# RWKV-7 block of a hybrid decoder trunk: small products regrouped by the part of TensorE's array that they use

## The chip, the cores and the metric

The kernel runs on one core of one Trainium2 chip. The metric is the device time of one execution in microseconds (us). Engines are named as in the profile: PE is TensorE (matmuls), PEld its weight loads, DVE VectorE, ACT ScalarE, POOL GpSimd, SP the engine that issues most DMAs. A difference of under about 0.2% (6 us) can't be told from no change here.

## The reference, cut to what matters

The trunk has two layers. Layer 0 runs two recurrent mixers side by side, RWKV-7 (8 heads of 64) and a gated delta rule (4 heads of 128), and adds their output projection to the stream; layer 1 is an RG-LRU; an MLP of width 4096 follows each. There are 1024 prompt tokens and 64 sample tokens (8 sequences of 8), width 1024, all in fp32. The change lies in RWKV-7 alone:

```
w_log = -softplus(-(w0 + tanh(xw) @ w2)) - 0.5        # decay: low-rank product, 64 -> 512
a     = sigmoid(a0 + xa @ a2)                         # in-context rate: low-rank product, 64 -> 512
per token t, per head:                                 # S is 64 x 64
  S = S * w_t + (S a_t) b_t^T + v_t k_t^T
  y_t = S r_t
```

The kernel doesn't go token by token. It cuts the tokens into chunks of 64 and, per chunk and head, works with 64x64 matrices: Gram matrices of (b, k) against (a, r), the inverse of a unit triangular one, u = -(I + L)^-1 x, the output y = (state part) + (part within the chunk), and the next state.

## The kernel before, in words

**Dense work.** Every large product (projections, output projection, MLPs) is made in `dense`: weights and activations are split into a high and a low part (`whi`, `wlo`, `xh`, `xl`), three 128x128 matmuls for each of eight 128-row tiles of the contraction, added in one PSUM bank. Tokens come in columns of 288 or 512.

**The stretch of the recurrences.** From about 270 us to 1130 us the two mixers' recurrences run in stages written out in `ORDER`: `r0 g0 r1 g1 ...`, where `r3` is RWKV's fourth block of 128 tokens, `g3` the delta rule's, and block 8 is the sample. Beside them runs dense work (second halves of the projections, then the output projection and the MLP's first half), which `tick` emits piece by piece. The small products and the dense ones go through the one queue of PE. Their order there is not the source's: the framework that compiles the kernel plans each engine's order beforehand, with the place in the source as priority and its own estimate of when operands and buffers are ready; on the chip each engine then works off its fixed order.

**One RWKV block** (`rwkv_block`, lines 1281 to 1457) treats all heads in lockstep. A pair of heads p (four pairs) shares the 128 partitions: head hh = 0 has partitions 0 to 63, hh = 1 has 64 to 127. A unit u is one chunk of 64 tokens of one pair, so a block of 128 tokens has eight units. Its products, each fp32 matmul of which stands in the trace as two records with a weight load each, are in order:

- decay (line 1316): for each pair, 64 rows of `wa2` (rows 0 to 63) times 128 feature columns, moving 128 tokens. ScalarE turns the bank into `cs`, which becomes the decays `ee`.
- in-context rate (line 1333), after a tick: the same with rows 64 to 127, into a bank of its own, then into `av`.
- Gram (line 1391): per unit and head one matmul with 64 rows and 128 columns ((b, k) by 64), moving 128 columns ((a, r) by 64); four units fill a bank for each head, and VectorE masks them into `ga` and `gr`.
- then `uv`, `xg`, the inverse (`blockinv` through DRAM, levels with `qq`, `tinv`), all in 64x64 products.

**The chain** (`rwkv_chain`, lines 1474 to 1499) then goes through the block's two chunks: xp = state times a (trace: `m<-st,ar`, 64 rows by 64 columns); the solve (`m<-xg,r`), whose result ACT and DVE write into `uv`; the state's increment sp (`m<-uv,bkt`, 128 by 64); two DVE operations that make the new state `st`; and the output y, pair by pair and head by head in one bank `yp`, where the state's part (`m<-ar,st`, 64 rows by 64 columns) is followed at once by the part within the chunk (`m<-gr,uv`, 128 rows by 64 columns).

Banks come from small pools: `psa` (2 banks) for the preparation of both mixers, `psb` (1) for the inverse's levels, `psc` (2) for the chain, `psp` (1) for y and what follows it, `psd` (2) for dense work. A bank is taken again when what reads it is done.

Of the kernel before, what the change touches and what calls it, by code (L numbers as in the profile page):

```python
# [18 lines left out]
P = 128  # L19
# [4 lines left out]
# order of the tokens: the prompt's first half, the sample, the prompt's second half  # L24
# [3 lines left out]
# chunks where the prompt comes first and the sample last  # L28
# [55 lines left out]
# tiles of the recurrences and of the work beside them: columns, ring  # L84
# [12 lines left out]
# tiles of the first MLP's middle that its first half has early: beside the recurrences, after them, in all  # L97
# [3 lines left out]
class Kern:  # L101
# [29 lines left out]
    def wpools(self, es, raw, parts):  # L131
        """places for raw weights and for their parts, beside those that are there"""
        k = len(self.wr)
        self.wr += [self.pool(es, f"wr{k}", raw)] * raw
        self.wp += [self.pool(es, f"wp{k}", parts)] * parts
        self.wn = self.wq = 0
# [9 lines left out]
    # ---- small helpers  # L146
# [9 lines left out]
    def mm(self, out, l, r, start=True, stop=True):  # L156
        return self.nc.tensor.matmul(out, l, r, start=start, stop=stop)  # L157
# [7 lines left out]
    # ---- set-up  # L165
# [10 lines left out]
    def setup_vec(self, vp):  # L176
        """parameters by feature, [P, .]"""
# [40 lines left out]
    def softplus(self, out, x, n, rows=P, pool=None):  # L218
        """out = max(x, 0) + log1p(exp(-|x|)), log1p as 2 atanh(u / (2 + u)); x is overwritten"""
        nc = self.nc  # L220
        pool = pool or self.cst
        ax = pool.tile([P, n], F32, name="spa")[:rows]
        u = pool.tile([P, n], F32, name="spu")[:rows]
        s2 = pool.tile([P, n], F32, name="sps")[:rows]
        self.stt(ax, x, -1.0, x, ALU.mult, ALU.max)
        self.act(u, ax, AF.Exp, scale=-1.0)
        nc.vector.tensor_scalar(ax, u, 2.0, None, op0=ALU.add)
        nc.vector.reciprocal(ax, ax)
        self.tt(u, u, ax, ALU.mult)
        self.tt(s2, u, u, ALU.mult)  # L230
        nc.vector.tensor_scalar(ax, s2, 2.0 / 17, 2.0 / 15, op0=ALU.mult, op1=ALU.add)
        for q in (13, 11, 9, 7, 5, 3, 1):
            self.tt(ax, ax, s2, ALU.mult)
            nc.vector.tensor_scalar(ax, ax, 2.0 / q, None, op0=ALU.add)
        self.tt(ax, ax, u, ALU.mult)
        self.stt(out, x, 0.0, ax, ALU.max, ALU.add)

    # ---- dense machinery
    def wload(self, src, kt, f):
        """src: DRAM [P, kt, f]; returns its two parts by k: [(hi [P, f], lo [P, f])]"""  # L240
        return self.wsplit(self.wraw(src, kt, f), f)
# [25 lines left out]
    def dense(self, w, f0, m, xs, c0, n, head=None):  # L267
        """sum_k w[:, k, f0:f0+m]^T x_k[:, c0:c0+n] into a bank, onto what head leaves there; c0:c0+n lies in
        one of the halves of x"""
# [14 lines left out]
    def xhalf(self, pool, n):  # L284
        """places for half of x_k: [(hi, lo)]"""
        return [tuple(pool.tile([P, n], F32R, name=f"x{p}{k}") for p in "hl") for k in range(8)]
# [13 lines left out]
    def r(self, c0, n):  # L300
        """factors of tokens c0.. of one half"""
        return self.rs[0][:, c0:c0 + n] if c0 < TA else self.rs[1][:, c0 - TA:c0 - TA + n]

    def norm(self, h, wname, l):
        """h times the weights of its norm, split, and in self.rs the factors by token, which the products of h with
        a matrix are still to be multiplied with"""
# [8 lines left out]
    def norm_half(self, hf, h, xs, i, wname, acc, tmp, parts):  # L315
        """half hf of it, in steps; h(f) is a tile of that half, which may be the place of its lower part"""
# [40 lines left out]
    # ---- input  # L357
# [24 lines left out]
    def norm_x(self, xi, h, xs):  # L382
        """first norm of half h of x, by token, and its transpose, split"""
# [36 lines left out]
    # ---- MLP  # L420
    def ahead(self, f0, f1):
        """tiles f0.. of the first MLP's middle, first half of the tokens, to DRAM"""
# [15 lines left out]
    def mlp(self, l, h, xs=None, early=0):  # L438
        """early: so many tiles of the middle lie in DRAM for the first half of the tokens"""
# [31 lines left out]
    # ---- output projection of a mixer: h[f] += sum over its feature tiles, in DRAM as ys [P, k, T]  # L471
    def outproj(self, w_out, xs, ys, h):
        """ys: DRAM [P, 8, T], the prompt first"""
# [15 lines left out]
    # ---- projected rows with their lead-in columns  # L489
    def evac(self, pp, psx, pre, ps, c0, n, b0=0, end=NP, rs=None):  # L490
        """bank of columns c0.. into the prompt tile [P, pre + tokens from b0] and, from column end on, the sample
        tile [P, 8, pre + 8]"""
# [13 lines left out]
    def rows_in(self, dst, src, nt, nr, pool=None):  # L506
        """dst [P, nt, nr] from DRAM rows [nr, nt * P]"""
# [9 lines left out]
    def rows_out(self, src, nt, nr, dsts, pool=None):  # L517
        """src [P, nt, nr] to DRAM rows; dsts: (first row, last row, DRAM rows [., nt * P])"""
# [10 lines left out]
    def tails(self, dst, t, pp, psx, k):  # L529
        """last k columns of the prompt and of each sequence into dst[:, t, :]"""  # L530
# [6 lines left out]
    # ---- RG-LRU layer  # L537
    def lru(self, h):
# [4 lines left out]
        # cL = -8 softplus(-L), stored halved  # L543
# [89 lines left out]
    def conv(self, out, pp, px, wname, nt, t, bias=None):  # L633
        """causal conv of one feature tile; out: tokens of the prompt, then those of the sample if px is there"""
# [13 lines left out]
    # ---- final norm and output  # L648
# [26 lines left out]
    # ---- layer 0: RWKV-7 and gated DeltaNet  # L675
    def scratch(self, name, cols, zero):
        """DRAM scratch for block inverses; zero: an SBUF tile of zeros to fill it with"""
# [5 lines left out]
    def blockinv(self, nb, lb, put, get):  # L683
        """inverses of unit lower 16-blocks, a block a partition: lb [nb, 16 (j), 16 (i)] holds the
        transposed blocks. Leaves them and their transposes in scratch; returns the loaded tiles"""
# [20 lines left out]
    def tick(self, n=1):  # L706
        """emits the next steps of the work that runs beside the recurrences"""
# [103 lines left out]
    def up_start(self):  # L811
        """the first MLP's norm for the first half of the tokens"""
# [9 lines left out]
    def shifted(self, h):  # L822
        """half h of the RWKV projections with their token shift"""
# [39 lines left out]
    def head_squares(self, t, o, m, ss, x):  # L863
        """adds to ss[:, o:o + m] the sums of squares by head that tile t brings; done when the result is called"""
# [13 lines left out]
    def gdn_bg(self):  # L878
        """the delta rule's write strengths and decays by head, to DRAM"""
# [7 lines left out]
    def silu(self, x):  # L887
        """x = y / 2 to y sigmoid(y)"""
# [4 lines left out]
    def delta_in(self, h):  # L893
        """half h of the delta rule's projections: rates, keys, queries and values with their convolution, gates"""
# [29 lines left out]
    def delta_z(self, h):  # L924
        """half h of the delta rule's gates"""
# [13 lines left out]
    def out_half(self, h):  # L939
        """half h of x and the output projection of both mixers, to DRAM"""  # L940
# [34 lines left out]
    def gdn_rates(self, sp):  # L975
        """by token, [P tokens, chunk, head]: write strengths, decays and their sums"""
# [67 lines left out]
    def gdn_block(self, n, b, X):  # L1044
        """everything of 128 tokens (64 of the sample) that needs no state; heads in lockstep"""
# [10 lines left out]
        # by token: keys, values; norms of keys and queries  # L1056
# [27 lines left out]
        # decays D[j, i], Gram matrices  # L1084
# [19 lines left out]
        # (I + N)^-1, transposed  # L1104
# [39 lines left out]
    def gdn_mid(self, b, R, X, p1, p2):  # L1144
        """from k S and q S by token (banks p1, p2): the new values, scaled for the state, and the output"""
# [67 lines left out]
    def gdn_post(self, b, R, X):  # L1213
# [13 lines left out]
        # with s = rq 128^-1/2: out = o s rsqrt(mean((o s)^2) + eps)  # L1227
# [15 lines left out]
    # RWKV: blocks of 128 tokens (64 of the sample), all heads in lockstep; a unit is 64 tokens of a pair of heads  # L1243
# [37 lines left out]
    def rwkv_block(self, n_, b, X):  # L1281
# [26 lines left out]
        # low-rank inputs  # L1308
# [4 lines left out]
        # decay  # L1313
        ps = self.bank()
        for p in range(4):
            self.mm(ps[:, p * n:(p + 1) * n], X["wa2"][:64, p * P:(p + 1) * P], rb[:64, 12])
# [13 lines left out]
        # in-context rate, keys  # L1330
        ps = self.bank()
        for p in range(4):
            self.mm(ps[:, p * n:(p + 1) * n], X["wa2"][64:, p * P:(p + 1) * P], rb[64:, 12])
        av, kk = flat("av"), flat("kk")
        for p in range(4):
            self.act(av[:, p * n:(p + 1) * n], ps[:, p * n:(p + 1) * n], AF.Tanh, bias=self.v("a0h", p), scale=0.5)
# [23 lines left out]
        # bonus  # L1360
# [8 lines left out]
        # values by token; the second head's before, the first head's after  # L1369
# [12 lines left out]
        # Gram matrices [(b|k) j, (a|r) i]; the second head has its k rows first  # L1382
# [3 lines left out]
        for u0 in range(0, U, 4):  # L1386
            gp = [self.bank(), self.bank()]
            for u in range(u0, u0 + 4):
                for hh in range(2):
                    r = slice(hh * 64, hh * 64 + 64)  # L1390
                    self.mm(gp[hh][:, (u - u0) * P:(u - u0 + 1) * P],
                            bk[r, u, hh:hh + 2, :].rearrange("p a t -> p (a t)"),
# [6 lines left out]
        # what the values bring to x  # L1399
# [6 lines left out]
        # b, k by token  # L1406
# [8 lines left out]
        # (I + L)^-1, transposed  # L1415
# [43 lines left out]
    def rwkv_solve(self, R, c, state):  # L1459
        """x = what the values (xg) and the state bring, u = -(I + L)^-1 x of a chunk of every pair, into its rows  # L1460
        of uv"""
# [12 lines left out]
    def rwkv_chain(self, R, st):  # L1474
# [3 lines left out]
        for c in range(2):  # L1478
# [11 lines left out]
            self.tt(sn, s1, lc.to_broadcast([P, 4, 64]), ALU.mult)  # L1490
            for p, hh, q in PH:
                self.mm(yp[q, (2 * p + c) * 64:(2 * p + c + 1) * 64], st[q, p, :], ar[q, 2 * p + c, 1, :], stop=False)
                self.mm(yp[q, (2 * p + c) * 64:(2 * p + c + 1) * 64], uv[:, p, c, hh, :], gr[:, hh, 2 * p + c, :],
                        start=False)
# [6 lines left out]
    def rwkv_states(self):  # L1501
        """states of the sequences for each pair of heads, [(h, k), s, v]"""
# [42 lines left out]
    def rwkv_update(self, R, sts):  # L1545
        """new states of the sequences"""
# [24 lines left out]
    def rwkv_post(self, R, y, X):  # L1571
        """group norm, bonus, gate"""
# [84 lines left out]
```

## Time and profile before

| | |
|---|---|
| Time of the kernel, three runs | 3003.88, 3005.15, 3005.59 us; median 3005.15 |
| The profiled execution | span 3000.1 us from its first to its last instruction; the median of the runs is 5.05 us more |
| PE busy | 2912.1 us, 97% of the span |
| PEld busy | 2549.8 us, 85% |
| DVE / ACT / POOL busy | 1582.5 us (53%) / 1133.3 us (38%) / 132.3 us (4%) |
| Mean granted TensorE clock | 0.980 of full |

Busy time counts an engine's instructions from start to end; a PE that is called busy can be filling and emptying its array between matmuls of different shape. So for PE the distance from one record's start to the next one's says more than the busy share.

### The profile page before, as it was taken

Reading aid. Unit: us, or ns where it says so; the run is one execution under the profiler, and the core shown is the slowest. Engines: PE = TensorE matmul, PEld = TensorE weight load, DVE = VectorE, ACT = ScalarE, POOL = GpSimd, SP = SyncE. Lnnn points to the kernel's source line nnn. Section 1 sums busy time; section 2 is a strip of 40 time slices with the busy share of each in tenths; the row PEclk is TensorE's granted clock in tenths of the full one; section 3 lists DMA queues with packets and bytes.
Section 4 is the critical chain, followed back from the end, with each engine's and each line's share of the span. In section 5 each row is a group of like instructions: output and inputs, shape, how many; then the busy total and the mean of one; then the engine's idle time right before and its main releaser. Section 6 shows DMA issues by size and latency. Waiting matters only on the chain. (4 is left out here: it accounts for less than half of the span.)

```text
span 3000.1 us, 49576 instructions
## 1 busy us (share of the span) xinstructions
PE 2912.1 (97%) x19772; PEld 2549.8 (85%) x19772; DVE 1582.5 (53%) x3383; ACT 1133.3 (38%) x2287; POOL 132.3 (4%) x337
## 2 busy tenths in 40 slices
PE   7999998999999999999999999999999999999997
PEld 6997776667787889988889999888889999999996
DVE  5375666577656563544444335677743333333335
ACT  6355444335345333522222224566441222222222
POOL 2111011110000000000000000000000000000000
PEclk9999998699999999999999999999999999999998
DMA  5344433344344335622221111121421111111112
GB/s 183 114 125 138 111 95 88 92 111 119 108 119 120 98 105 165 197 86 73 79 73 58 46 44 43 47 70 55 150 67 44 43 49 43 43 50 43 43 57 88
DMA packets 419661, 261.04 MB, mean 87 GB/s; under 512 B 95205, under 2 KB 390943, under 8 KB 419430
## 3 DMA queue, kind: packets, MB, share of 16 engines
q1 hardware_dynamic: 413302, 241.90, 27.9%
q0 software_dynamic: 5696, 14.86, 1.6%
q8 instruction: 155, 2.54, 0.3%
q10 hardware_dynamic: 432, 1.11, 0.1%
q14 instruction: 76, 0.62, 0.1%
HBM read 204.07 MB, written 53.73 MB: 86 GB/s over the span
## 5 line engine op out<-in xcount | busy, mean ns | idle before, releaser
L157 PE MATMUL m<-xh,whi 128*128 128x288 f32 (+3 forms) x2984 | 992.1, 333 | 4.6 <-DVE big L151 1.4
L157 PE MATMUL m<-xl,whi 128*128 128x288 f32 (+3 forms) x2984 | 991.4, 333 | 1.3 <-DVE xl L154 0.9
L157 PE MATMUL m<-xh,wlo 128*128 128x288 f32 (+3 forms) x2984 | 981.9, 330 | 0.2
L157 PE MATMUL m<-big,whi 128*128 128x288 f32 (+1 forms) x3072 | 723.2, 327 | 0.0
L148 ACT ACTIVATE whi<-wraw 128x512 fp32r<-128x512 f32 x525 | 329.2, 629 | 1028.1 <-PE m L157 966.9
L157 PEld LDWEIGHTS m<-xh,whi 128*128 128x128 f32 (+1 forms) x2984 | 562.5, 189 | 53.6 <-issue 2.1
L157 PEld LDWEIGHTS m<-xl,whi 128*128 128x128 f32 (+1 forms) x2984 | 563.1, 189 | 44.8 <-issue 1.7
L157 PEld LDWEIGHTS m<-xh,wlo 128*128 128x128 f32 (+1 forms) x2984 | 563.0, 189 | 43.0 <-issue 1.0
L157 PEld LDWEIGHTS m<-big,whi 128*128 128x128 f32 x3072 | 520.2, 188 | 40.4
L151 DVE TENSOR_TENSOR wlo<-wraw,whi 128x512 fp32r<-128x512 f32 x525 | 359.3, 686 | 327.4 <-ACT whi L148 318.4
L157 PE MATMUL m<-big,wlo 128*128 128x288 f32 (+1 forms) x1536 | 501.0, 326 | 0.0
L151 DVE TENSOR_TENSOR h<-h,m 128x288 f32<-128x288 f32 (+1 forms) x408 | 217.0, 532 | 361.9 <-PE m L157 361.9
L157 PEld LDWEIGHTS m<-big,wlo 128*128 128x128 f32 x1536 | 288.3, 188 | 20.6
L148 ACT ACTIVATE mid<-mid 128x288 f32<-128x288 f32 (+1 forms) x202 | 104.1, 518 | 240.3 <-DVE mid L154 203.9
L154 DVE SCALAR_TENSOR_TENSOR mid<-m,rs 128x512 f32<-128x512 f32 (+1 forms) x154 | 85.4, 555 | 177.7 <-PE m L157 177.7
L151 DVE TENSOR_TENSOR big<-mid,big 128x288 fp32r<-128x288 f32 (+2 forms) x170 | 99.4, 585 | 119.8 <-ACT big L148 119.4
L148 ACT ACT_TABLE_LOAD x68 | 87.2, 1283 | 27.9 <-DVE tbtmp L151 13.2
L148 ACT ACTIVATE big<-mid 128x288 fp32r<-128x288 f32 (+2 forms) x170 | 92.7, 545 | 6.5 <-DMA mid<-ma 1.5
L154 DVE SCALAR_TENSOR_TENSOR fpo<-fpp,vt,fpo 128x512 f32<-128x512 f32 x100 | 74.5, 745 | 30.9 <-ACT fpo L148 26.2
L148 ACT ACTIVATE fpp<-m 128x288 f32<-128x288 f32 (+1 forms) x78 | 34.9, 449 | 64.9 <-PE m L157 56.6
L151 DVE TENSOR_TENSOR tbtmp<-lb,tb 32x15 f32<-32x15 f32 (+8 forms) x270 | 51.3, 190 | 5.9 <-DMA lb<-rs 1.6
L151 DVE TENSOR_TENSOR tb<-tb,tbtmp 32x15 f32<-32x15 f32 (+8 forms) x270 | 51.8, 192 | 4.3
(387 smaller groups left out, 2716.9 us busy)
## 6 DMA issues: line engine op xcount, KB each, us to landing
wraw<-mlp_up SPq DMA_DIRECT2D x172, 256.0 KB
wraw<-mlp_down SPq DMA_DIRECT2D x136, 256.0 KB
wraw<-w_in_even SPq DMA_DIRECT2D x120, 256.0 KB
wraw<-w_out_even SPq DMA_DIRECT2D x32, 256.0 KB
wraw<-w_in_odd SPq DMA_DIRECT2D x32, 256.0 KB
wraw<-w_out_odd SPq DMA_DIRECT2D x32, 256.0 KB
in<-rd SPq DMA_DIRECT2D x8, 896.0 KB
mid<-ma SPq DMA_DIRECT2D x22, 288.0 KB
```

Of the source, the lines that this page charges most:

```text
L148: return self.nc.scalar.activation(out, in_, f, **kw)
L151: return self.nc.vector.tensor_tensor(out, a, b, op)
L154: return self.nc.vector.scalar_tensor_tensor(out, a, s, b, op0, op1, **kw)
L157: return self.nc.tensor.matmul(out, l, r, start=start, stop=stop)
```

## The change

Three groups of RWKV's small products are regrouped; what is computed stays the same.

- y: the eight state parts of a chunk go first, in one run, and the eight parts within the chunk after them, in a second run. All sixteen add into one bank, of which only the block's first matmul of each head clears the marks (`start`).
- Gram: each 64x128 product becomes two of 64x64, and they are issued as four quarters of the array: (head 0, b), (head 1, k or b), (head 0, k), (head 1, the other).
- low rank: decay and in-context rate are made in one place, as 64x64 quarters in the same order, into two banks that are taken together; the bank of the rate is read where it was made before.

```diff
-    def mm(self, out, l, r, start=True, stop=True):
-        return self.nc.tensor.matmul(out, l, r, start=start, stop=stop)
+    def mm(self, out, l, r, start=True, stop=True, **kw):
+        return self.nc.tensor.matmul(out, l, r, start=start, stop=stop, **kw)
...
-        ps = self.bank()
+        ps, psr = self.bank(), self.bank()
         for p in range(4):
-            self.mm(ps[:, p * n:(p + 1) * n], X["wa2"][:64, p * P:(p + 1) * P], rb[:64, 12])
+            for k, m in ((0, 0), (1, 1), (0, 1), (1, 0)):
+                f, h64 = p * P + m * 64, slice(k * 64, k * 64 + 64)
+                self.mm((ps, psr)[k][m * 64:(m + 1) * 64, p * n:(p + 1) * n], X["wa2"][h64, f:f + 64], rb[h64, 12])
...
-        ps = self.bank()
-        for p in range(4):
-            self.mm(ps[:, p * n:(p + 1) * n], X["wa2"][64:, p * P:(p + 1) * P], rb[64:, 12])
         av, kk = flat("av"), flat("kk")
         for p in range(4):
-            self.act(av[:, p * n:(p + 1) * n], ps[:, p * n:(p + 1) * n], AF.Tanh, bias=self.v("a0h", p), scale=0.5)
+            self.act(av[:, p * n:(p + 1) * n], psr[:, p * n:(p + 1) * n], AF.Tanh, bias=self.v("a0h", p), scale=0.5)
...
             for u in range(u0, u0 + 4):
-                for hh in range(2):
+                for hh, k in ((0, 0), (1, 1), (0, 1), (1, 0)):
                     r = slice(hh * 64, hh * 64 + 64)
-                    self.mm(gp[hh][:, (u - u0) * P:(u - u0 + 1) * P],
-                            bk[r, u, hh:hh + 2, :].rearrange("p a t -> p (a t)"),
+                    self.mm(gp[hh][k * 64:(k + 1) * 64, (u - u0) * P:(u - u0 + 1) * P], bk[r, u, hh + k, :],
                             ar[r, u].rearrange("p a t -> p (a t)"))
...
+            cols = lambda p: slice((2 * p + c) * 64, (2 * p + c + 1) * 64)
             for p, hh, q in PH:
-                self.mm(yp[q, (2 * p + c) * 64:(2 * p + c + 1) * 64], st[q, p, :], ar[q, 2 * p + c, 1, :], stop=False)
-                self.mm(yp[q, (2 * p + c) * 64:(2 * p + c + 1) * 64], uv[:, p, c, hh, :], gr[:, hh, 2 * p + c, :],
-                        start=False)
+                self.mm(yp[q, cols(p)], st[q, p, :], ar[q, 2 * p + c, 1, :], start=(c == 0 and p == 0), stop=False,
+                        skip_group_check=True)
+            for p, hh, q in PH:
+                self.mm(yp[q, cols(p)], uv[:, p, c, hh, :], gr[:, hh, 2 * p + c, :], start=False,
+                        skip_group_check=True)
```

The rest of the difference is comments that were taken out.

## Rows read from the trace of the kernel before

**Rows 1.** The profile's page: busy engines, then PE and its clock in 40 slices.
```profile
PE 2912.1 (97%) x19772; PEld 2549.8 (85%) x19772; DVE 1582.5 (53%) x3383; ACT 1133.3 (38%) x2287; POOL 132.3 (4%) x337
...
PEclk9999998699999999999999999999999999999998
```
**Rows 2.** Busy time by stretch, with granted clock, DMA share, GB/s at the end.
```profile
270.00:420.00 150.00, 148.65 (x1304) 113.86 (x1304) 96.29 (x264) 74.11 (x182) 13.76 (x27) 1.00 0.43 110
420.00:660.00 240.00, 215.13 (x1496) 154.92 (x1495) 155.46 (x429) 95.88 (x233) 35.91 (x63) 0.85 0.36 90
660.00:1140.00 480.00, 464.80 (x4383) 399.70 (x4383) 308.31 (x847) 215.44 (x544) 20.83 (x37) 0.98 0.43 116
```
**Rows 3.** Who waited for whom, 260 to 1140 us: total, times, longest.
```profile
PE m L157 <- DVE fpp L525: 6.0, 1, 6.0
...
ACT whi L148 <- PE m L157: 76.8, 40, 6.0
ACT uv L148 <- PE m L157: 67.7, 21, 8.2
```
**Rows 4.** Timeline of PE, one chunk's end: start, us, instruction, count of records.
```profile
337.99 0.68 PE L157 MATMUL m<-uv,bkt 128*64 128x64 f32 x14
338.51 0.28 PE L157 MATMUL m<-gr,uv 128*64 128x64 f32 x2
...
339.23 0.33 PE L157 MATMUL m<-ar,st 64*64 64x64 f32 x2
339.48 0.33 PE L157 MATMUL m<-gr,uv 128*64 128x64 f32 x2
339.74 0.33 PE L157 MATMUL m<-ar,st 64*64 64x64 f32 x2
...
341.80 0.50 PE L157 MATMUL m<-xh,wlo 128*128 128x512 f32 x1
342.14 0.40 PE L157 MATMUL m<-xh,whi 128*128 128x512 f32 x1
342.46 0.68 PE L157 MATMUL m<-st,ar 64*64 64x64 f32 x16
342.98 0.28 PE L157 MATMUL m<-ar,st 64*64 64x64 f32 x2
...
343.52 0.39 PE L157 MATMUL m<-xh,wlo 128*128 128x512 f32 x1
343.76 0.39 PE L157 MATMUL m<-xh,whi 128*128 128x512 f32 x1
```
**Rows 5.** Records of PE by tile: count, ns min/median/max, first and last start.
```profile
L157 PE MATMUL m<-gr,uv x272: 221/222/271, 337.1 to 1069.7; 128*64 128x64 f32 x136
...
L157 PE MATMUL m<-ar,bk x272: 271/272/374, 284.4 to 1013.2; 64*128 64x128 f32 x136
...
L157 PE MATMUL m<-in,wa x144: 271/272/524, 271.2 to 965.8; 64*128 64x128 f32 x128, 64*128 64x64 f32 x16
```
**Rows 6.** Timeline of PE: the first block's Gram products.
```profile
284.42 1.86 PE L157 MATMUL m<-ar,bk 64*128 64x128 f32 x16
286.20 0.49 PE L157 MATMUL m<-xh,whi 128*128 128x512 f32 x1
286.63 1.71 PE L157 MATMUL m<-ar,bk 64*128 64x128 f32 x16
288.27 0.50 PE L157 MATMUL m<-xl,whi 128*128 128x512 f32 x1
```
**Rows 7.** Timeline of PE: the second block's low-rank products and what ran between.
```profile
316.17 1.16 PE L157 MATMUL m<-in,wa 64*128 64x128 f32 x8
317.25 0.50 PE L157 MATMUL m<-xh,whi 128*128 128x512 f32 x1
...
322.32 1.14 PE L157 MATMUL m<-tinv,ga 64*64 64x64 f32 x30
...
325.21 1.16 PE L157 MATMUL m<-in,wa 64*128 64x128 f32 x8
326.29 0.91 PE L157 MATMUL m<-qq,tinv 64*64 64x64 f32 x24
```
**Rows 8.** Timeline of DVE: the new state, between sp and xp.
```profile
338.71 0.42 DVE L151 TENSOR_TENSOR s<-m,st 128x256 f32<-128x256 f32 x1 [0.47 <-PE m L157]
...
339.17 0.42 DVE L151 TENSOR_TENSOR st<-s,lam 128x256 f32<-128x256 f32 x1
```

## The prediction

> **What bounds the kernel now.** I read the page first: PE is busy for 97% of the span, DVE for 53% [rows 1]. So time is gained where PE's queue becomes shorter, and the question is whether that holds in the stretch that the change touches, 270 to 1140 us. The windows say that it does: PE is busy for 148.65 + 215.13 + 464.80 = 828.6 of 870 us there, and DVE, the next, for 560 [rows 2]. The waits agree: the longest single wait of PE is 6.0 us, while ACT alone waits 76.8 us for PE to let go of a weight tile and 67.7 us for a solve's result [rows 3]. The 41 us in which PE is not busy lie mostly in 420 to 660 us, round the sample block, where the granted clock is 0.85, that is, part of the stretch runs at the lower of the two levels [rows 2]. I did not trust the busy share further than that, and read the timeline record by record, from start to start, since a busy PE can be one that fills and empties its array.
>
> **y in two runs.** In the timeline of a chunk's end the two shapes of y alternate, two records of one, two of the other. Such a double pair takes 339.74 - 339.23 = 0.51 us for four records, 128 ns each. The same 64x64 shape in an unbroken run takes (342.98 - 342.46) / 16 = 32 ns a record, and the 128x64 shape (338.51 - 337.99) / 14 = 37 ns [rows 4]. So three quarters of y's time is the change of shape and two passes of one product that wait for each other. There are 8 blocks x 2 chunks x 8 = 128 such pairs (272 records of the second part, less 16 of the sample, are 256 [rows 5]), so y costs 128 x 0.51 = 66 us. After the change a chunk has 16 records at 32 ns and 16 at 37 ns, 1.1 us, and at most one more change of shape than now, 0.2 us (dense matmuls follow one another after 343.76 - 343.52 = 0.24 us, and after 0.34 and 0.32 us next to a run of another shape; so a change costs some 0.1 us, and a visit, with both, 0.2 to 0.25 [rows 4]). That is 1.3 us against 4.1, 16 times: 45 us saved. Bounds: if both runs stand next to products of their own shape (xp is 64x64, sp 128x64), nothing is added and 49 us are saved; if the planner cuts each run into three with dense work between, four more visits of 0.25 us a chunk leave 29 us.
>
> **Gram.** A block has two visits of 16 records. The first takes 286.20 - 284.42 = 1.78 us, 112 ns a record: the two heads, which use different rows of the array, stand behind one another; in the second 1.64 us [rows 6]. A record loads 128 columns and streams 128 (112 ns); a 64x64 record of the run above does so with 64 and 64, two places at a time, so about 60 ns for each [rows 4]. A quarter loads 64 and streams 128, so I estimate 86 ns, and each old record becomes two. If the two column halves of one head run side by side, as two 64-column products do in the 37 ns run, 272 records [rows 5] become 272 slots of 86 instead of 112 ns: 7 us saved, which I take, because it assumes only what rows show (columns side by side) and no more of the heads' overlap than there is now. Bounds: all four side by side, 136 x 86 ns = 12 us, against 272 x 112 = 30: 18 saved; all behind one another, 544 x 86 = 47: 16 lost.
>
> **Low rank.** Here 144 records [rows 5], 8 to a visit where decay and rate stand apart, 317.25 - 316.17 = 1.08 us each [rows 7]; at 112 ns a record they come to 16 us and the visits' own cost. After: one visit a block; 144 slots of 86 ns are 12 us if column halves alone overlap, 6 us if the rows do too, 25 us if nothing does; and up to 9 visits fewer save about 0.2 us each, 2 us. I take 8 us saved, between 4 + 2 and 10 + 2; bounds 12 saved, 7 lost. The rate's product moves ahead of a tick, past the dense work that the tick emits, from 325.21 to 316.17 in the second block [rows 7]. Its operands are there, as they come by the same load; its reader stays where it was. What it costs is a bank of `psa` held for 9 us longer; the next claim on it comes after the rate's reader anyway, so I cost it at nothing, and what it costs if that is wrong is the second rival below.
>
> **What then is late.** PE reaches the next chunk's xp earlier, and xp needs the new state. DVE makes it from 338.71 to 339.17 + 0.42 = 339.59 [rows 8], and xp starts at 342.46. With the second run of y done 0.6 us after 338.51, and the two dense matmuls between, 0.66 us, PE would be there at 339.8: just enough [rows 4]. Where fewer or shorter dense matmuls stand there PE waits some tenths; I allow 0.3 us for each of 16 chunks, 5 us. No DMA and no instruction of DVE, ACT or POOL is added.
>
> **Sum.** 45 + 7 + 8 - 5 = 55 us off the span of 3000.1, which makes 2945; the median of the runs is 5 us above the span, so 2950 us.
>
> Two rules of the Trainium skill stand against each other here. The 32 ns run shows two quarters in flight, no more [rows 4]. The page "TensorEngine Tiling (Array Packing)", section "Performance Considerations", under "Instruction Overhead", says that each matmul has some 60 cycles of overhead on trn2 and that one should not tile a dimension that is already small; as an estimate from that page, 416 added records at 25 ns would be 10 us, and the sum 45 instead of 55. The page "TensorE: Matmul & The Clock Gate", Part 3, says instead that tiles in different rows and columns run together, a few ns apart; by it Gram and low rank reach their upper bounds and the sum would be 70. No row here shows four quarters in flight; both results lie within the forecast's own range below.
>
> **Rivals.**
> 1. The gain is half taken back. Were the stretch to keep its 870 us, PE with 60 us less would be busy for 88% of it, and DVE (560 us) and the chain through solve, DVE and PE set more of the pace; for it speaks that PE does wait round the sample, 41 us in all [rows 2]; against it, that the others wait for PE far more than it for them [rows 3]. Half of 55 gone: 2977 us.
> 2. The time becomes longer: `psa` stands still. Both its banks are taken at the block's start and one is read only after the tick; the delta rule's preparation lives on the same two banks. If everything that needs `psa` stands while the rate's bank is held, the price is up to 325.21 - 316.17 = 9 us in each of 9 blocks, 81 us against 60: 3026 us. It decides from 60 / 9 = 6.7 us a block. For it: the pool has two banks, and an RWKV block's preparation claims a bank of it eleven times. Against it: in those 9 us PE ran dense work and the inverse's products, from other pools [rows 7].
> 3. The quarters run behind one another. Then Gram loses 16 and low rank 7, y gains 45, 5 are lost to waits: 17 saved, 2988 us. For it: the Gram products of the two heads, though on different rows, take 112 ns a record as if alone in the array [rows 6]; against it: the 37 ns run of two column halves [rows 4].
> 4. The planner cuts the runs of y apart, so that the change doesn't do what it says: y gains 10 at most, the rest 15 less the waits: 2985 us. For it: of the 16 records of sp only 14 stand together, two were placed elsewhere [rows 4]; against it: the 16 of xp are in one run [rows 4].
>
> **How the numbers follow.** The forecast 0.65 (its own range 2925 to 2965); rival 1 0.15; rival 2 0.07; rival 3 0.07; rival 4 0.06. The range goes from 2925 (upper bounds of y, Gram and low rank, 49 + 18 + 12 = 79) to 2985 (rival 1 and part of 3 and 4), and leaves out rival 2, most of 3, half of 4 and the forecast's tails. Under about 6 us, 0.2%, nothing can be told from no change: faster 0.90 (forecast, rivals 1, 3, 4 less a little), same 0.04, slower 0.06.
>
> **What would show it.** In the trace after: y's two tiles each as runs of 16 records at 32 and 37 ns, the 16 chunks' y together at about 20 us; Gram's records at some 43 ns apart (86 for two), or 21 if all four quarters run; one visit of `wa` products a block with 32 records in 1.4 us or less; PE's waits between 260 and 1140 us up by 5 us and not by 30. The prediction is wrong if y's runs are cut, if two quarters of one head start 86 ns apart instead of together, if the claims on `psa` show up as waits of PE on ACT at `av`, or if waits round the sample grow by what PE gained.

## The result, and the profile after

The changed kernel takes 2956.9 us in the median of four runs (2950.6 to 2962.8) against 3004.5 us before, a ratio of 0.983 (95% interval 0.981 to 0.986). In a second comparison it was 2952.5 against 3006.6 us, 0.981 (0.979 to 0.984). So 48 to 54 us went; the forecast was 55.

The profiled execution has a span of 2955.4 us, 44.7 less than before; it ran at a mean granted clock of 0.977 and the one before at 0.980, so this difference is rather on the low side of what the medians show. The page of after: PE is busy for the same share as it was [rows 1], with 416 more records and 54 us less of busy time.

```profile
span 2955.4 us, 50421 instructions
...
PE 2857.9 (97%) x20188; PEld 2506.8 (85%) x20188; DVE 1584.2 (54%) x3383; ACT 1126.8 (38%) x2281; POOL 126.6 (4%) x337
...
PEclk9999999779999999999999999999999999999998
```

All of it comes from the stretch of the recurrences. The last of the delta rule's products (`m<-bkt,gr`) starts at 1082.7 us instead of 1128.4, 45.7 us earlier; what follows is as long as before, within 1 us. The windows of after, with the columns of [rows 2]:

```profile
270.00:420.00 150.00, 146.04 (x1502) 112.43 (x1503) 102.11 (x287) 74.79 (x188) 14.85 (x27) 1.00 0.45 115
420.00:660.00 240.00, 211.93 (x1650) 148.22 (x1648) 163.94 (x429) 95.37 (x236) 33.45 (x68) 0.84 0.38 98
660.00:1093.00 433.00, 414.65 (x4445) 363.55 (x4445) 296.67 (x824) 208.87 (x530) 13.80 (x30) 0.98 0.45 121
```

The timeline of PE over one chunk's end and the next one's start answers to [rows 4]. y's second part is now 13 records behind sp's, its first part 16 records behind xp's, each next to products of its own shape:

```profile
868.83 0.27 PE L157 MATMUL m<-gr,uv 128*64 128x64 f32 x1
868.88 0.22 PE L157 MATMUL m<-uv,bkt 128*64 128x64 f32 x1
868.93 0.64 PE L157 MATMUL m<-gr,uv 128*64 128x64 f32 x13
869.50 0.41 PE L157 MATMUL m<-xh,wlo 128*128 128x320 f32 x1
...
870.42 0.68 PE L157 MATMUL m<-st,ar 64*64 64x64 f32 x16
870.93 0.63 PE L157 MATMUL m<-ar,st 64*64 64x64 f32 x16
871.50 0.41 PE L157 MATMUL m<-xl,whi 128*128 128x320 f32 x1
```

For the parts' cost I add up, over all records of a tile, the time from each record's start to the start of the next one on PE. This charges a group with the change of shape behind it, and with a wait if one falls there.

| us on PE, start to start | before | after | forecast |
|---|---|---|---|
| y (`m<-ar,st` and `m<-gr,uv`) | 65.2 (0.7 of it waits) | 23.4 | -45 |
| Gram (`m<-ar,bk`) | 31.2 | 29.9 (2.3 of it waits) | -7 |
| low rank (`m<-in,wa`) | 21.4 | 16.2 (2.7 of it waits) | -8 |
| waits of PE for other engines, 260 us to the stretch's end | 45.1 | 53.9 | +5 |

A wait of PE that falls behind a record stands both in the record's group and in the last line, so the lines can't simply be added. Without the waits y fell by 41.1 us, Gram by 3.7 and low rank by 7.9, 53 in all; with 1 us of other records, and less the 9 us by which the waits grew, that is the 45 us of the span. So y and low rank brought about what they should and Gram half, and the waits grew by 9 us instead of 5. The Gram products of the first block after, which answer to [rows 6], show what became of them: 32 quarters in one visit, but 1.72 us in the first (287.67 - 285.95) and 1.12 in the second.

```profile
285.95 1.79 PE L157 MATMUL m<-ar,bk 64*64 64x128 f32 x32
287.67 0.50 PE L157 MATMUL m<-xh,whi 128*128 128x512 f32 x1
...
289.26 1.18 PE L157 MATMUL m<-ar,bk 64*64 64x128 f32 x32
290.38 1.02 PE L157 MATMUL m<-fpp,ct 128*8 128x512 f32 x2
```

And the second block's low-rank products, which answer to [rows 7], in one visit of 1.03 us where there were two of 1.08:

```profile
316.92 1.10 PE L157 MATMUL m<-in,wa 64*64 64x128 f32 x32
317.95 0.50 PE L157 MATMUL m<-xh,whi 128*128 128x512 f32 x1
```

### The profile page after: what moved, and what is told of

Read it like the earlier page. It is cut to its first block, busy times and chain, and to the rows that moved or that the text cites. A ratio compares the mean times of both kernels' runs of the same rounds, so it can differ in the third digit from the quotient of the medians.

```text
span 2955.4 us, 50421 instructions
## 1 busy us (share of the span) xinstructions
PE 2857.9 (97%) x20188; PEld 2506.8 (85%) x20188; DVE 1584.2 (54%) x3383; ACT 1126.8 (38%) x2281; POOL 126.6 (4%) x337
```

## The experiments

Runs of one and the same kernel lie up to 25 us apart here, so first how to read their times. The 23 runs of the kernel before that stood beside the first four experiments go from 3001.6 us, at a mean granted clock of 0.980, to 3020.0, at 0.974; over the 23, time falls by 2.75 us for each 0.001 of clock (correlation -0.93). In the profiles before and after, the largest part of the time at the lower level lies round the sample block, where PE waits (a mean clock of 0.85 and 0.84 in 420 to 660 us); where it falls differs from run to run. I therefore list, beside each median, the mean over the runs of time times granted clock: what would be left if PE had worked at full clock and were the bound all through. That is a working and not a measurement; with a clock given to 0.001 it is good to some 2 us. Each ratio is to runs of the kernel before on the same chip; beside `after_again` and the parts in pairs these had a median of 3006.6 us, beside `y_pairs_one_shape` and `after_ticks` 3009.0.

| kernel | runs | median us | ratio to before (95%) | mean clock | time x clock |
|---|---|---|---|---|---|
| before (beside the first four) | 23 | 3009.9 | | 0.9767 | 2940 |
| after | 4 | 2956.9 | 0.983 (0.981 to 0.986) | 0.9773 | 2890 |
| after_again | 5 | 2952.5 | 0.981 (0.979 to 0.984) | 0.9794 | 2892 |
| y_only | 4 | 2973.1 | 0.988 (0.987 to 0.990) | 0.9765 | 2904 |
| gram_only | 12 | 3015.3 | 1.0015 (0.9998 to 1.0031) | 0.9742 | 2936 |
| low_only | 12 | 3009.6 | 0.9996 (0.9979 to 1.0014) | 0.9766 | 2939 |
| y_gram | 5 | 2960.7 | 0.984 (0.982 to 0.987) | 0.9806 | 2903 |
| y_low_quarters | 5 | 2958.1 | 0.983 (0.981 to 0.986) | 0.9796 | 2898 |
| y_low_rows | 4 | 2960.6 | 0.984 (0.982 to 0.986) | 0.9800 | 2901 |
| y_low_rows_t | 6 | 2968.6 | 0.986 (0.983 to 0.988) | 0.9782 | 2900 |
| y_pairs_one_shape | 4 | 2978.9 | 0.989 (0.986 to 0.992) | 0.9763 | 2908 |
| after_ticks | 6 | 2966.7 | 0.985 (0.983 to 0.988) | 0.9770 | 2898 |

### Each part alone

`y_only`: the last hunk of the change and the new arguments of `mm`, nothing else.

> The kernel before with y alone in two runs of eight; Gram and low-rank products as before. Theory (the gain is y's change of shape, which the other two parts neither need nor help): y's 512 records take 23 us instead of 65, as they do with all three parts, so about 2963 us (2957 to 2968). Rival (the waits of PE take half of it back, and it is the other two parts that keep PE's queue short enough): 2975 us or more, with the waits of PE between 260 and 1140 us up by some 20 us.

Measured 2973.1 us, 37 less than before. y took 23.4 us (13.8 and 9.6), as in the whole change, so 41.8 us of PE went. Theory held as to y; the time lies 5 us above the theory's range and just below the rival's 2975. The waits of PE rose from 45 to 55 us, by 10 and not by 20.

`gram_only`: the Gram hunk alone.

> The kernel before with the Gram products alone as 64x64 quarters. Theory (a record holds its place in the array for the time of its streamed columns, 109 ns for 128 of them, and the load of its weights is hidden; so a quarter takes as long as a 64x128 product and there are twice as many): Gram's 544 records take 28 to 32 us against 31, and the time is 3004 us within 5. Rival (the prediction's price, 86 ns for a quarter and two column halves side by side): 24 us and 2997 us. Second rival (quarters one behind another): 47 us and 3020 us.

Measured 0.9998 to 1.0031 of before: no gain that can be told. Gram's 544 records took 29.5 us against 31.2, inside what the theory gave and far from both rivals' 24 and 47. The median is 5 us up, and its clock is the lowest in the table, 0.9742; by time x clock it is 4 us down.

`low_only`: the two low-rank hunks alone.

> The kernel before with the low-rank products alone as 64x64 quarters in one place. Theory (all four quarters run at once, eight places of 109 ns a block, and one visit of PE instead of two): 21 us become 16 and the time is 2999 us, 2995 to 3003. Rival (the bank of the rate, held longer, makes the other users of the two banks wait): 3006 us or more, with PE waiting for ACT where it did not before.

Measured 0.9979 to 1.0014, no change: the theory's 2999 did not come, and 3009.6 lies where the rival had it. The products themselves became cheaper: of the 22.1 us that the sum charges to them, 9.4 are waits of PE, and 12.7 are left of 21.4. The time did not follow. 9.0 of those 9.4 us are a single wait, behind the visit at 478.7 us in the sample's block, and the profile puts it down to ACT's `av`, which reads the rate's bank, as the rival would have it. But it ends with the delta rule's transposes `m<-ct,bkt` at 488.44 us, which write a bank of `psp` and not of `psa`, and whose operand DVE wrote until 488.29. So that the rate's bank held anything up is not shown. In the kernel before PE waits in the same block, for 6.0 us, ahead of the low-rank products [rows 3]; the visit seems to have moved ahead of that wait, which stayed. The waits rose to 59 us in all, and why they rose stays open.

### How the low-rank products have to stand

`y_low_rows`: y in runs, Gram as before, decay and rate side by side as 64x128 products:

```diff
         ps, psr = self.bank(), self.bank()
         for p in range(4):
-            for k, m in ((0, 0), (1, 1), (0, 1), (1, 0)):
-                f, h64 = p * P + m * 64, slice(k * 64, k * 64 + 64)
-                self.mm((ps, psr)[k][m * 64:(m + 1) * 64, p * n:(p + 1) * n], X["wa2"][h64, f:f + 64], rb[h64, 12])
+            for k in range(2):
+                h64 = slice(k * 64, k * 64 + 64)
+                self.mm((ps, psr)[k][:, p * n:(p + 1) * n], X["wa2"][h64, p * P:(p + 1) * P], rb[h64, 12])
```

> y in two runs, decay and rate in one place but as 64x128 products that alternate between the array's two row halves (16 records a block, not 32 quarters), Gram as before. Theory (what runs side by side is what stands on different rows, whatever its columns): a block's 16 low-rank records take 0.9 to 1.1 us as the 32 quarters do, and the time is that of the kernel after within 5 us, 2952 to 2962. Rival (only quarters run side by side, 64x128 products on different rows stand behind one another as the Gram products before seemed to): 1.7 us a block, 6 us more than the quarters in all, 2963 us or more.

Measured 2960.6 us, in the theory's range. In its timeline 16 records take 318.85 - 317.76 = 1.09 us, as the 32 quarters do in 1.03:

```profile
317.76 1.16 PE L157 MATMUL m<-in,wa 64*128 64x128 f32 x16
318.85 0.50 PE L157 MATMUL m<-xh,whi 128*128 128x512 f32 x1
```

So products need not be quarters to run side by side: it is enough that they stand on different halves of the rows and are issued alternately. Over all nine blocks, without the waits behind them, the low-rank records take 14.6 us here, 20.9 in `y_only` and 12.3 as quarters (`y_low_quarters`, below); what the quarters bring beyond the place is 2 us, less than the times can tell. Of the 12 us of time over `y_only`, 3 stand in time x clock; the rest goes with the clock (0.9800 and 0.9765).

### Parts in pairs

`after_again` (the changed kernel), `y_gram` (without the low-rank hunks), `y_low_quarters` (without the Gram hunk) and `y_low_rows_t` ran on one chip. The last is the row version with this edit more:

```diff
-        for hh, q, qo in HR:
-            ps = self.bank()
-            for u in range(U):
-                nc.tensor.transpose(ps[:, u * 64:(u + 1) * 64],
+        tp = [self.bank(), self.bank()]
+        for u in range(U):
+            for hh, q, qo in HR:
+                nc.tensor.transpose(tp[hh][:, u * 64:(u + 1) * 64],
                                     bk[q, u, hh:hh + 2, :].rearrange("p a t -> p (a t)"), self.c("ident")[q, q])
-            self.act(bkt[:, hh], v64(ps[:, :N]))
+        for hh, q, qo in HR:
+            self.act(bkt[:, hh], v64(tp[hh][:, :N]))
```

> The changed kernel once more, to be compared on one chip with its parts. Ratio to the kernel before 0.981 to 0.986; single runs spread over 12 us or more, with the granted clock between 0.975 and 0.980, about 3 us per 0.001.

> y in two runs and Gram as quarters, low rank as before. Theory (a quarter holds its place as long as a 64x128 product, so Gram's regrouping brings 1 to 2 us of PE's time whatever stands beside it): the ratio of y alone, 0.988, within 0.002. Rival (64x64 quarters lie between other 64x64 products without a change of shape once y is in runs, and so bring 10 us that they did not bring alone): 0.985 or less.

> y in two runs and low rank as quarters, Gram as before. Theory (the step from y alone to the whole change is the low-rank products' place, one visit a block ahead of the tick, and Gram brings nothing): the ratio of the whole change and of the row version, 0.984 within 0.002. Rival (all of it is how the planned order and the free-running clock fall, and no part of it is the low-rank products'): 0.988, as y alone.

> As the row version (y in two runs, decay and rate as 64x128 products alternating between the row halves), and the transposes of b and k by token also alternate between the two heads, into two banks, where one head's stood behind the other's. Theory (what stands on different rows runs side by side): these 136 records take 6 to 8 us instead of 11.5, and the time falls by 3 to 5 us against the row version, ratio 0.982 to 0.983. Rival (the second bank taken at once makes the delta rule's preparation wait, or the planner orders them one head after the other again): 0.984 or more.

The changed kernel came out a little better than forecast from its first runs, and again spread with the clock (2959.9 us at 0.978, 2946.1 at 0.981). `y_gram` fell outside what I expected of the theory: 0.984, as the rival had it. But not by the rival's way: its Gram products took 30.7 us, against 32.1 in `y_only`, 1.4 less, and its time x clock is that of `y_only`, 2903 and 2904. What it has over `y_only` is clock, 0.9806 against 0.9765, from fewer stretches at the lower level round the sample block; the windows at 600 to 660 us of the two, clock in the third place from the end, show one of them:

```profile
600.00:660.00 60.00, 54.05 (x341) 37.45 (x340) 47.07 (x108) 20.33 (x43) 14.04 (x24) 0.91 0.36 92
```

```profile
600.00:660.00 60.00, 53.92 (x413) 39.04 (x409) 49.52 (x119) 27.11 (x64) 12.06 (x22) 1.00 0.42 104
```

The first is `y_only`, the second `y_gram`. `y_low_quarters` came at 0.983 as its theory said; 6 us of its 15 over `y_only` stand in time x clock, the rest is clock again (0.9796).

`y_low_rows_t` missed, as its rival had it: its transposes took 11.6 us, as before. The timeline shows why: the planned order puts the eight of one head first and a dense matmul between them and the other eight, whatever the order in the source.

```profile
289.71 0.71 PE L1410 MATMUL m<-ct,bk 64*128 64x64 f32 x8
290.35 0.50 PE L157 MATMUL m<-xh,wlo 128*128 128x512 f32 x1
290.77 0.71 PE L1410 MATMUL m<-ct,bk 64*128 64x64 f32 x8
```

That its median is 8 us above the row version is clock (0.9782 against 0.9800); time x clock is the same, 2900 and 2901.

### What y's time was

`y_pairs_one_shape` keeps y's order pair by pair and takes away the change of shape:

```diff
-                self.mm(yp[q, (2 * p + c) * 64:(2 * p + c + 1) * 64], st[q, p, :], ar[q, 2 * p + c, 1, :], stop=False)
+                self.mm(yp[q, (2 * p + c) * 64:(2 * p + c + 1) * 64], uv[:, p, c, hh, :], gr[:, hh, 2 * p + c, :],
+                        stop=False)
```

> The kernel before with y pair by pair as it was, but the state's part of y is replaced by a second product of the part within the chunk, so that both products of a pair have 128 rows and 64 columns: the alternation and the adding into the same columns stay, the change of shape goes (y lacks the state's part and has the other twice). Theory (the change of shape is what y's time was): the 528 records of y take 25 to 32 us instead of 65, and the time is 2970 to 2978 us, ratio 0.987 to 0.991, as for y alone in two runs. Rival (two products into the same columns of a bank, one after the other, wait for each other whatever their shape): 55 us or more and 2995 us or more.

Its y, 528 records, took 21.8 us, below even the theory's range; its time is that of `y_only` (0.989 and 0.988). In its timeline a chunk's 32 records of y take 344.43 - 343.35 = 1.08 us, alternating as before in what they add to, but all of one shape; before, such a chunk took 4.1 us [rows 4]:

```profile
342.83 0.69 PE L157 MATMUL m<-uv,bkt 128*64 128x64 f32 x16
343.35 1.15 PE L157 MATMUL m<-gr,uv 128*64 128x64 f32 x32
344.43 0.38 PE L157 MATMUL m<-gS,ar 128*128 128x128 f32 x1
```

So y's extra time was the change of shape between 64x64 and 128x64, not the adding into the same columns. The rival fell.

### What a quarter costs

`gram_moving_halves` cuts the Gram products along the other side, same weights, half the moving columns:

```diff
-                    self.mm(gp[hh][:, (u - u0) * P:(u - u0 + 1) * P],
-                            bk[r, u, hh:hh + 2, :].rearrange("p a t -> p (a t)"),
-                            ar[r, u].rearrange("p a t -> p (a t)"))
+                    for k in range(2):
+                        o = (u - u0) * P + k * 64
+                        self.mm(gp[hh][:, o:o + 64], bk[r, u, hh:hh + 2, :].rearrange("p a t -> p (a t)"),
+                                ar[r, u, k, :])
```

> The kernel before with each Gram product cut along its moving side: the same 64x128 weights loaded twice, 64 columns streamed each time, so 544 records that load 128 columns and stream 64, where the quarters load 64 and stream 128. Theory (a place in the array is held for the streamed columns alone): consecutive records of one head start 56 to 64 ns apart and the Gram products take 30 to 34 us, as they do in one piece or in quarters. Rival (loading and streaming add up, as the prediction's 86 ns assumed, which gives the same 86 ns here): 82 to 90 ns apart and 42 to 47 us in all. The time is one look and decides nothing.

Both theories fell. Records of one head start 112 ns apart, as with 128 moving columns; Gram took 51.9 us (one run: 3051.8 us beside 3010.9). Its first visit, 32 records in 286.71 - 283.84 = 2.87 us:

```profile
283.84 2.94 PE L157 MATMUL m<-ar,bk 64*128 64x64 f32 x32
286.71 0.50 PE L157 MATMUL m<-xh,whi 128*128 128x512 f32 x1
```

Together with the quarters (load 64, stream 128: consecutive records of one quarter start 109 ns apart in the visit of 285.95 in the profile after) and with the products of 64 by 64 (58 ns), this gives one reading that fits all four: for these fp32 records a place in the array is held for the longer of loading and streaming, not for their sum and not for the streaming alone.

### More dense work beside the sample

`after_ticks` is the changed kernel with `self.tick()` behind each pair in `rwkv_update`.

> The changed kernel with one more tick behind each pair of heads in the update of the sample's states, four in all, so that four more dense tiles are emitted beside the sample block. Theory (what the kernels of this study differ by beside their products is the time at the lower clock level round the sample block, some 30 us of it for every 0.005 of mean clock): the mean granted clock rises from 0.978 to 0.981 or more and the time falls to a ratio of 0.977 to 0.980. Rival (the low stretches there come from the delta rule's sample products, which wait for DVE whatever dense work is at hand, or the tiles are missing in the stages behind): clock 0.977 to 0.979 and the changed kernel's own ratio, 0.981 to 0.984, or worse.

The rival held: clock 0.977, ratio 0.985, no better than the changed kernel. Four more dense tiles emitted there did not raise the mean clock; what makes the low stretches stays open. No version of this study beats the changed kernel: `y_gram`, `y_low_quarters` and the row version come within their intervals of it.

## Why the prediction was right, and where it was off

**PE bounds the stretch: right.** Without its waits PE's work in the three groups became shorter by 53 us (41.1 + 3.7 + 7.9), and the span by 44.7. The forecast's 55 us were added up from the profiled span, where 45 came; the medians of the runs fell by 48 to 54, which is nearer to it in part by luck, as the profiled execution of before had the higher clock.

**y: right, mechanism and size.** 45 us forecast, 41.8 measured; `y_pairs_one_shape` shows that it was the change of shape. The wait of a product's two passes for each other, which the prediction named beside it, went with it: their starts lay 107 ns apart in the alternation, and 58 ns is the distance of records in one place in `y_pairs_one_shape`. Of the 3 us, 2 are that a chunk took 4.0 us before and not 4.1; it takes 1.4 and not 1.3 after, as the planner still places records apart from the run, like the one at 868.83 in the timeline above. Rival 4, runs cut so far apart that y gains 10 at most, did not come.

**Gram: the step that failed.** "A quarter loads 64 and streams 128, so I estimate 86 ns" added loading and streaming up. The trace after has 109 ns, and `gram_moving_halves` shows the same price, 112, with the two swapped. So a quarter is hardly cheaper than the 64x128 product it halves, and the assumed overlap of the two column halves gives back just what their number costs. That the two heads stand behind one another was a misreading too: it holds for the first block, which the prediction read, but later in the same trace of before 16 uncut records of two heads take 849.46 - 848.37 = 1.09 us, and 32 quarters take 1.03 at best.

```profile
848.37 1.16 PE L157 MATMUL m<-ar,bk 64*128 64x128 f32 x16
849.46 0.71 PE L157 MATMUL m<-ct,fth 128*128 128x128 f32 x4
```

So cutting bought no overlap that the uncut products could not have. The 3.7 us that Gram gained fit visits in which both heads' quarters are in flight: 1.12 us for 32 in the second visit, 1.64 for 16 before. In the first visit the first weight load that waits for a semaphore of its own, 0.70 us after the visit's start, is read as the second head's, held for its bank; so little is gained there. Rival 3, quarters one behind another, would have made 47 us of it, and it was 30.

**Low rank: the 8 us came, in part by luck.** In the second block one visit of 1.03 us took the place of two of 1.08, as forecast, and without the waits 21.4 us became 13.5. But two errors offset each other in it: a quarter costs 109 ns and not 86, and all four run side by side, where the forecast took a value between two and four. The 2.7 us of waits in the sum stand mostly in the sample's own block, where the visit at 474.54 us is cut by a wait of PE for DVE (1.60 us) and followed by one for a DMA (0.76).

```profile
474.54 0.68 PE L157 MATMUL m<-in,wa 64*64 64x64 f32 x16 [2.08 <-DVE fpp L525]
476.83 1.12 PE L157 MATMUL m<-in,wa 64*64 64x64 f32 x16 [1.60 <-DVE fpp L525]
478.71 0.47 PE L157 MATMUL m<-tinv,ga 64*64 64x64 f32 x2 [0.76 <-DMA tinv<-rs]
```

The bank of the rate, held longer, showed up in no wait of PE for `av`; rival 2 did not come.

**What then is late: right, without the cost.** From the end of the new state to the start of the next xp there were 2.6 to 3.0 us before, and are 0.2 to 0.6 us after, in all eight blocks; PE is recorded as waiting for it in none. The cover of 2.3 us is gone, and a state that came more than 0.2 to 0.6 us later would now make PE wait. The 5 us that I had put there came, as 9, elsewhere, spread over waits of which the longest is 4.5 us.

**What 416 more records cost.** The added records cost nothing that shows: 32 quarters in 1.03 us stand against 16 products in 1.09. So the 60 cycles or so of overhead per matmul that the Trainium skill's page "TensorEngine Tiling (Array Packing)" states under "Instruction Overhead" do not come on top here, as the quarters overlap. The first two quarters of the visit at 285.95 start 7 ns apart, so do the first two low-rank products on different rows at 317.76 in `y_low_rows`, and in the visit at 289.26 four quarters start in each 109 ns, once it runs. That agrees with the Trainium skill's page "TensorE: Matmul & The Clock Gate", Part 3, which has tiles in different rows and columns run together, a few ns apart. But the sum of 70 that followed from it with the price of 86 ns did not come.

**What stays open.** The parts' gains don't add. In time x clock, each value good to some 2 us, Gram's quarters bring 4 us alone, 1 beside y, and 7 beside y and low rank (2898 to 2891); the low-rank part brings 1, 6 and 12 in the like places. Each edit makes the planner order the whole stretch anew, dense matmuls and the other mixer's products with it, and with the order goes the time at the lower clock round the sample (0.91 and 1.00 in the windows of `y_only` and `y_gram` above). Which order falls out well was not settled. After all, 37 of the 48 to 54 us are shown to be y's; the other 11 to 17 are shown only as what the two other parts bring together with it.

## What to carry to other kernels

Where products of different array shapes alternate, read the timeline from start to start: a pair that takes several times what the same shapes take in runs is time that grouping by shape gives back, and here 37 of the 42 us came off the total. Cutting a product into smaller tiles gains only where something else can then stand beside it: look first whether the same products, uncut, can be issued alternately on different rows. And before two versions a few tenths of a per cent apart are compared, look at each run's granted clock.

## What the runs showed of the hardware

- A change between a 64x64 and a 128x64 shape, with two records of each, cost 128 ns a record; in runs of one shape the same records take 32 and 37 ns.
- Uncut fp32 products on different halves of the rows, issued alternately, start 5 to 7 ns apart and run side by side: 16 in 1.09 us, where decay's and rate's, not alternated, took 1.64 in the first block of the kernel before (271.20 us).
- An fp32 record of this kernel holds its place for about the longer of loading and streaming: 58 ns for 64 and 64 columns, 109 for 64 and 128, 112 for 128 and 64, 112 for 128 and 128.
- The mean granted clock of one and the same kernel went from 0.973 to 0.980 over 23 runs, and the time with it by 18 us.
